# A PEER expert mixer on one core: the first head of the gathered tokens ranked in a batch of its own, its row gathers issued during the query projections, and three U blocks loaded there into a tile of their own

## The chip, the cores and the metric

The kernel runs on one core of a Trainium2 chip. The metric is the device time of one execution in microseconds (us). Engines: PE multiplies matrices, DVE (VectorE), ACT (ScalarE) and POOL (GpSimd) compute elementwise, SP only issues DMAs here. Each engine works through its instructions in the order in which they stand in its program; instructions on different engines wait for each other by semaphores.

## The reference, cut to what matters

The step handles 336 rows of width 1024: 256 prompt tokens, 64 sample tokens and 16 meta tokens. A trunk layer (convolution and state-space branches) comes first and is untouched by the change. Behind it 320 tokens go through a PEER mixer:

```python
def peer_block(xb, w_q, keys, U, V):
    q = (xb @ w_q).reshape(T, PEER_HEADS, 2, D_KEY // 2)       # 8 heads, 2 halves of 128
    s = jnp.einsum('thcd,hckd->thck', q, keys).astype(jnp.float32)   # 128 keys each
    s1, i1 = lax.top_k(s[:, :, 0], PEER_TOPK)                  # 16 best of each half
    s2, i2 = lax.top_k(s[:, :, 1], PEER_TOPK)
    cand = (s1[..., :, None] + s2[..., None, :]).reshape(T, PEER_HEADS, PEER_TOPK * PEER_TOPK)
    sc, f = lax.top_k(cand, PEER_TOPK)                         # 16 experts of 16384 per head
    ids = (jnp.take_along_axis(i1, f // PEER_TOPK, axis=-1) * N_KEYS
           + jnp.take_along_axis(i2, f % PEER_TOPK, axis=-1))
    g = jax.nn.softmax(sc, axis=-1)
    act = jax.nn.gelu(jnp.einsum('thkd,td->thk', U[ids], xb).astype(jnp.float32), approximate=False)
    w = (g * act).astype(xb.dtype)
    return jnp.einsum('thk,thkd->td', w, V[ids])
```

U and V have 16384 rows of 1024 floats, 64 MB each. Per token, 8 × 16 = 128 rows of each are used.

## The kernel before, in words

Two ways lead through the mixer, and both run at once.

**Gathered tokens.** The first 128 tokens (`NGAT`) fetch their own rows. A column is one of the 128 (head, rank) pairs; for each, one indirect DMA issued by POOL (line 1081) brings the row of U and V of every token, 128 × 2048 floats, into one of `UV` = 5 buffers named `wuv`. A *row look* (`pick_dot`, line 1193) is one DVE instruction that multiplies the U half with the token and sums it; ACT makes the Gelu of the sum and scales it (1195, 1196). A *row sum* (`pick_sum`, line 1201) is one DVE instruction that adds the scaled V half to `ygat`. 16 more columns hold the 16 meta tokens, so there are 144 gathers.

**Dense tokens.** The other 176 tokens (`ND`) go through all of U in 128 blocks of 128 experts: a 512 KB load by SP into a ring of eight buffers (`eraw`, line 1262), eight fp32 matmuls (`u_block`, line 1270; 16 matmul rows in the profile), a Gelu on ACT into `S` (1272). Then `S` is multiplied with gates, which PE builds from one-hot matrices (`pg`, `g_step`), and 128 blocks of V follow in the same manner (`va`, line 1364). The 16 choices of each of these tokens (the top-k of tiles 1 and 2, tile 2 with the meta tokens) are found by *background tasks* on DVE, mixed with the row looks while the U blocks run. At the end of a tile's ranking stands `look`, which ends in `pick` (line 1047); then PE transposes the picks (*placement*, `pix`, line 1161). A placement is tied behind a U block of a fixed number, `PLACE` = (38, 50) counted from 0.

**Before the blocks** come the 16 query projections, one per head and half (loop at line 1095): a 512 KB weight load, a cast `wh` on ACT (218), the rest `wl` on POOL (219), 24 matmuls, the copy `qT`, three score matmuls `psc` (1103) and copies of the scores (1105). DVE finds the 16 best of the gathered tokens at once (`top16`, line 995 ff.). `heads(h0)` then ranks the candidates of four heads in a batch of 26 DVE instructions and an Exp, and writes the row numbers `gid` and the weights `ggw`. Behind the first batch, with j = 7, `ahead(0)` issues the first gathers. The background top-k of tile 1 and 2 from score 6 on is tied behind the first batch's numbers (`early[0]`).

A scheduler with a simulated timeline decides the order in which each engine's instructions stand, from this recorded code, its waits and a few ties such as those of the placements. At the end, behind V block 126 (`LASTP`), `finish` normalises and writes the gathered tokens (`out_y`, line 1359), in tiles taken from the ring; `finish_dense` writes the others.

Of the kernel before, what the change touches and what calls it, by code (L numbers as in the profile page):

```python
# [7 lines left out]
F32 = mybir.dt.float32  # L8
# [13 lines left out]
PJ = 512  # L22
T = TP + NQ * TS
# [113 lines left out]
def body(tc, ia, oa, stop=None):  # L137
    nc = tc.nc
    with ExitStack() as top:
        cp = top.enter_context(tc.tile_pool(name="cp", bufs=1))  # L140
        ps = top.enter_context(tc.tile_pool(name="ps", bufs=1, space=bass.MemoryType.PSUM))
# [59 lines left out]
        def pj2(name="pj"):  # L201
            return pj(name)[:, :T2]
# [55 lines left out]
        def misc(shape, name):  # L258
            return ps.tile(shape, F32, name=name, tag="misc", bufs=2)
# [631 lines left out]
        for j in range(KD):  # L891
# [4 lines left out]
            p = pj2()  # L896
# [23 lines left out]
        p = ps.tile([128, T], F32, name="pn2", tag="pb", bufs=1)  # L920
# [9 lines left out]
        nd = gp.tile([128, KD, ND], F32, name="nd")  # L930
# [16 lines left out]
        kp = ks.enter_context(tc.tile_pool(name="kp2", bufs=1))  # L947
# [9 lines left out]
        for c_ in range(2):  # L957
            p = misc([128, 512], "px")
# [4 lines left out]
        p = misc([128, 4], "prs")  # L963
# [7 lines left out]
        if NX:  # L971
# [18 lines left out]
        keys = qp.tile([128, 16, NK], F32, name="keys")  # L990
# [14 lines left out]
        sv = [kp.tile([128, 16, 16], F32, name=f"sv{i}") for i in range(3)]  # L1005
        si = [kp.tile([128, 16, 16], U32, name=f"si{i}") for i in range(3)]
        sall = kp.tile([128, 2, 16, NK], F32, name="sall")
        cv0 = kp.tile([128, PH, 16], F32, name="cv0")
        ci0 = kp.tile([128, PH, 16], U32, name="ci0")

        def candidates(L, H_, s2):
            c = kp.tile([128, PH * 136], F32, name="cand", bufs=1)[:L]
            cf = c[:, :H_ * 136].rearrange("p (h n) -> p h n", h=H_)
            nc.vector.tensor_tensor(cf[:, :, :16], s2[:, :, 0, 0:1].to_broadcast([L, H_, 16]), s2[:, :, 1, :],
                                    op=OP.add)
            nc.vector.tensor_tensor(cf[:, :, 16:].rearrange("p h (a b) -> p h a b", b=8),
                                    s2[:, :, 0, 1:, None].to_broadcast([L, H_, 15, 8]),
                                    s2[:, :, 1, None, :8].to_broadcast([L, H_, 15, 8]), op=OP.add)
            return c, cf

        def table(L, H_, idx):
            sf = kp.tile([128, PH, 2, 16, 4], BF, name="sf", bufs=2)[:L, :H_]
            nc.vector.tensor_copy(sf.rearrange("p h c k t -> p (h c k) t"),
                                  idx.rearrange("p h k -> p (h k)")[:, :, None].to_broadcast([L, H_ * 32, 4]))
            return sf

        def places(L, H_, f):
            lo = kp.tile([128, PH * 16], U32, name="plo")[:L, :H_ * 16]
            rr = kp.tile([128, PH * 16], U32, name="prr")[:L, :H_ * 16]
            ab = [kp.tile([128, PH * 16], BF, name=f"pab{c_}")[:L, :H_ * 16] for c_ in range(2)]  # L1030
            nc.vector.tensor_scalar(lo, f, 7, None, op0=OP.bitwise_and)
            nc.vector.tensor_scalar(rr, f, 3, None, op0=OP.logical_shift_right)
            nc.vector.tensor_scalar(ab[0], rr, 1.0, 0.0, op0=OP.subtract, op1=OP.max)
            nc.vector.tensor_scalar(ab[1], rr, 1.0, 8.0, op0=OP.is_equal, op1=OP.mult)
            nc.vector.tensor_tensor(ab[1], ab[1], lo, op=OP.add)
            return ab

        def look(out, L, H_, at, sf, half, c):
            e = c.bitcast(BF)[:, :H_ * 256].rearrange("p (g a t) -> p g a t", a=16, t=4)
            nc.vector.tensor_tensor(e, at.rearrange("p (g t) -> p g t", t=4)[:, :, None, :].to_broadcast(  # L1040
                [L, H_ * 4, 16, 4]), iorep[:L, None, :16].to_broadcast([L, H_ * 4, 16, 4]), op=OP.is_equal)
            m = e.rearrange("p (h q) a t -> p h q (a t)", h=H_)
            nc.vector.tensor_tensor(m, m, sf[:, :, half].rearrange("p h k t -> p h (k t)")[:, :, None].to_broadcast(
                [L, H_, 4, 64]), op=OP.mult)
            for w in (8, 4, 2):
                nc.vector.tensor_tensor(e[:, :, :w], e[:, :, :w], e[:, :, w:2 * w], op=OP.add)  # L1046
            nc.vector.tensor_tensor(out.rearrange("p (g t) -> p g t", t=4), e[:, :, 0], e[:, :, 1], op=OP.add)

        early = []

        def heads(h0):
            hs_ = slice(h0, h0 + HG)
            cs = slice(16 * h0, 16 * (h0 + HG))
            sf = table(128, HG, si[0][:, 2 * h0:2 * h0 + 2 * HG])
            c, cf = candidates(128, HG, sv[0].rearrange("p (h c) k -> p h c k", c=2)[:, hs_])
            for h in range(HG):
                top16(cv0, ci0, cf[:, h], h0 + h)
            ab = places(128, HG, ci0.rearrange("p h k -> p (h k)")[:, cs])
            pk = kp.tile([128, 2, HG * 16], F32, name="pkh")
            for half in range(2):  # L1060
                look(pk[:, half], 128, HG, ab[half], sf, half, c)
            idf = kp.tile([128, HG * 16], F32, name="idh")
            nc.vector.scalar_tensor_tensor(idf, pk[:, 0], float(NK), pk[:, 1], op0=OP.mult, op1=OP.add)
            early.append(nc.vector.tensor_copy(gid[:, cs], idf).ins.name)
            g_ = kp.tile([128, HG, 16], F32, name="gh")
            nc.vector.tensor_tensor(g_, cv0[:, hs_], cv0[:, hs_, 0:1].to_broadcast([128, HG, 16]), op=OP.subtract)
            act(g_, g_, AF.Exp, scale=rsT[:, 0:1])
            sm = kp.tile([128, HG], F32, name="smh")
            nc.vector.tensor_reduce(sm, g_, axis=AX.X, op=OP.add)
            nc.vector.reciprocal(sm, sm)  # L1070
            nc.vector.tensor_tensor(ggw[:, cs].rearrange("p (h k) -> p h k", k=16), g_,
                                    sm[:, :, None].to_broadcast([128, HG, 16]), op=OP.mult)

        COLS = list(range(XAT)) + list(range(NPICK, NCOL)) + list(range(XAT, NPICK))
        pend = {}
# [1 line left out]
        ustep, vstep = [], []  # L1077

        def gather(c):
# [10 lines left out]
        def ahead(n):  # L1090
            for i_ in range(n, min(n + UV - 1, NCOL)):
                if i_ not in pend:
                    pend[i_] = gather(COLS[i_])

        for j in range(16):
            w = weight(ia["w_q"], j)
            p = pj()
            proj(p[:, :T2], w, rows(ah[:, :, :T2], al[:, :, :T2]))
            qT = qp.tile([128, T], F32, name="qT", bufs=3)
            nc.scalar.copy(qT[:, :T2], p[:, :T2])  # L1100
            p = misc([128, 3, NK], "psc")
            for i, (t0, L) in enumerate(KTILES):
                nc.tensor.matmul(p[:L, i], qT[:, t0:t0 + L], keys[:, j, :], start=True, stop=True)
                s_ = sall[:, i - 1, j] if i else kp.tile([128, NK], F32, name="sco", bufs=9)
                nc.scalar.copy(s_[:L], p[:L, i])
                if i == 0:
                    top16(sv[i], si[i], s_[:L], j)
            if j % (2 * HG) == 2 * HG - 1:
                heads(j // 2 - HG + 1)
            if j == 2 * HG - 1:  # L1110
                ahead(0)
        qs.close()
        xs.close()
        s0p = top.enter_context(tc.tile_pool(name="s0p", bufs=1, side=RIGHT))
# [145 lines left out]
        def block(src, i):  # L1260
            raw = ring()
            nc.sync.dma_start(raw, src[i])
            return raw.rearrange("p (k m) -> p k m", k=KD)

        def u_block(b):
            raw = block(ia["uT"], b)
            tag, nb = (("pj", 3), ("y", 2), ("pj", 3), ("y", 2), ("pj", 3), ("pb", 1))[b % 6]
            p = ps.tile([128, PJ], F32, name="pj", tag=tag, bufs=nb)[:, :T]
            for k in range(KD):
                i_ = nc.tensor.matmul(p[:, :ND], raw[:, k, :], nd[:, k, :], start=(k == 0), stop=(k == KD - 1))  # L1270
            ustep.append(i_.ins.name)
            nc.scalar.activation(Sv(b), p[:, :ND], AF.Gelu)  # L1272

        def after(i_, name):
# [223 lines left out]
```

## Time and profile before

| | |
|---|---|
| median of 3 runs | 1377.38 us (1375.13 to 1377.93) |
| the profiled execution's own time | 1379.1 us |
| its span in the profile | 1377.3 us |
| mean granted clock of PE | 0.988 |
| PE busy | 1317.0 us (96%) |
| DVE busy | 1015.0 us (74%) |
| ACT, POOL busy | 529.9, 580.0 us |
| moved by DMA | 382 MB, mean 277 GB/s |

All rows of a profile are of one execution; its own time is the one that sums are set against, and it stands 1.7 us above the median. The trunk fills the first 560 us or so, the query projections lie from about 560 to 655, the U blocks from there on, and the V blocks end at about 1365. Busy shares over the whole span say little here, since each stage has a limit of its own: windows of one stage, and the waits within it, are what to read.

### The profile page before, as it was taken

The numbers are of one execution on the slowest core, as the hardware profiler recorded it, in microseconds if no ns is written. First come the engines' busy times: TensorE is split into PE (matmuls) and PEld (weight loads), VectorE is DVE, ScalarE is ACT, GpSimd is POOL, SyncE is SP. The second block draws the span as 40 slices with busy tenths as digits, with TensorE's granted clock in tenths as the row PEclk, the third lists the DMA queues.
The fourth block names the chain that finished last, engine by engine and source line by source line (L and its number), as shares of the span: only waits on it lengthen the run. The fifth ranks groups of instructions, "written<-read, shape, count | busy, mean of one in ns | idle before, by whom it ended". The sixth has DMA issues, their size and how long they took to land.

```text
span 1377.3 us, 24605 instructions
## 1 busy us (share of the span) xinstructions
PE 1317.0 (96%) x9328; PEld 1244.9 (90%) x9328; DVE 1015.0 (74%) x2339; ACT 529.9 (38%) x1411; POOL 580.0 (42%) x477
## 2 busy tenths in 40 slices
PE   9899999999999999998998998999999999986997
PEld 7788888988889999898998998999999999976997
DVE  6787778877877246789999986668787777766533
ACT  6687877778666444343232221111111111111101
POOL 1386777776665667542212332123221212344210
PEclk9899999999999999999999999999999999999999
DMA  6435454444434544638999999899999999999993
GB/s 234 143 120 175 154 177 131 157 162 164 133 121 133 158 144 153 190 93 329 411 415 391 402 416 410 303 417 359 370 415 413 384 370 378 407 417 416 414 411 104
DMA packets 87094, 382.05 MB, mean 277 GB/s; under 512 B 10144, under 2 KB 15648, under 8 KB 66368
## 3 DMA queue, kind: packets, MB, share of 16 engines
q1 hardware_dynamic: 65056, 227.46, 45.9%
q0 software_dynamic: 20736, 151.00, 27.1%
q10 hardware_dynamic: 1184, 2.02, 0.4%
q8 instruction: 73, 1.20, 0.4%
q14 instruction: 45, 0.37, 0.1%
HBM read 367.41 MB, written 13.03 MB: 276 GB/s over the span
## 4 chain that ended last, share of the span: by engine, by line
PE 74%; DVE 14%; DMA 10%; ACT 1%; issue 0%; POOL 0%; DVEq 0%; ACTq 0%; SPq 0%; POOLq 0%
PE pj L151 31%; PE va L1364 17%; PE pj L1270 11%; DMA eraw<-in_vE_dram 7%; PE pg L1299 4%; DMA eraw<-in_uT_dram 3%; PE pst L151 2%; DVE ygat L1201 2%; DVE wuv L1193 2%; PE po L151 1%; PE py L151 1%; PE pdec L151 1%; PE ptr L156 1%; DVE cand L1046 1%; PE pq L151 1%; DVE si L1003 1%
## 5 line engine op out<-in xcount | busy, mean ns | idle before, releaser
L1081 POOL DMA_INDIRECT wuv<-in_peer_uv_dram,gid x144 | 187.7, 1303 | 513.2 <-DVE ygat L1201 149.1
L219 POOL TENSOR_TENSOR wl<-wraw,wh 128x1024 fp32r<-128x1024 f32 x111 | 267.0, 2407 | 178.0 <-ACT wh L218 96.6
L1364 PE MATMUL va<-S,eraw 128*128 128x176 f32 x2048 | 317.7, 315 | 19.9 <-DMA eraw<-in_vE_dram 19.9
L1364 PEld LDWEIGHTS va<-S,eraw 128*128 128x128 f32 x2048 | 306.0, 190 | 27.5 <-DMA eraw<-in_vE_dram 24.4
L1270 PE MATMUL pj<-nd,eraw 128*128 128x176 f32 x2048 | 318.9, 315 | 12.0 <-ACT S L1272 6.6
L1270 PEld LDWEIGHTS pj<-nd,eraw 128*128 128x128 f32 x2048 | 307.6, 191 | 15.1 <-ACT S L1272 9.3
L151 PE MATMUL pj<-ah,wh 128*128 128x336 f32 (+1 forms) x768 | 244.3, 329 | 2.5 <-ACT xg L194 2.2
L151 PE MATMUL pj<-al,wh 128*128 128x336 f32 (+1 forms) x768 | 234.4, 318 | 0.0
L1201 DVE SCALAR_TENSOR_TENSOR ygat<-wuv,scg,ygat 128x1024 f32<-128x1024 f32 x128 | 164.1, 1282 | 57.3 <-ACT scg L1196 57.1
L1195 ACT ACTIVATE scg<-scg 128x1 f32<-128x1 f32 x144 | 29.1, 202 | 420.0 <-DVE wuv L1193 419.9
L1193 DVE SCALAR_TENSOR_TENSOR wuv<-wuv,x2m 128x1024 f32<-128x1024 f32 x128 | 156.2, 1221 | 38.9 <-DMA wuv<-in_peer_uv_dram,gid 38.9
L218 ACT CAST wh<-wraw 128x1024 fp32r<-128x1024 f32 x125 | 131.3, 1051 | 119.0 <-PE pj L151 81.0
L472 DVE SCALAR_TENSOR_TENSOR pcv<-ccat,vec,pcv 128x256 f32<-128x256 f32 x464 | 148.9, 382 | 15.1 <-ACT pcv L470 15.1
L151 PEld LDWEIGHTS pj<-ah,wh 128*128 128x128 f32 x768 | 147.4, 192 | 10.4 <-issue 2.6
L151 PEld LDWEIGHTS pj<-al,wh 128*128 128x128 f32 x768 | 147.0, 192 | 0.7
L151 PE MATMUL pj<-ah,wl 128*128 128x336 f32 (+1 forms) x768 | 137.5, 316 | 0.0
L151 PEld LDWEIGHTS pj<-ah,wl 128*128 128x128 f32 x768 | 121.1, 189 | 0.9 <-issue 0.7
L1272 ACT ACTIVATE S<-pj 128x176 f32<-128x176 f32 x128 | 37.5, 312 | 145.0 <-PE pj L1270 145.0
L1299 PE MATMUL pg<-oh 128*128 128x64 bf16 x1056 | 74.9, 241 | 0.0
L1299 PEld LDWEIGHTS <-oh 128*128 128x128 bf16 x1056 | 70.8, 117 | 2.0
L1306 DVE TENSOR_TENSOR S<-S,pg 128x192 f32<-128x192 f32 (+1 forms) x66 | 31.6, 507 | 54.3 <-PE pg L1299 54.3
L486 DVE SCALAR_TENSOR_TENSOR pj<-mcat,vec,pj 128x360 f32<-128x360 f32 x96 | 56.6, 591 | 3.7 <-ACT pj L484 3.7
(363 smaller groups left out, 1709.4 us busy)
## 6 DMA issues: line engine op xcount, KB each, us to landing
eraw<-in_uT_dram SPq DMA_DIRECT2D x128, 512.0 KB, 11.0
eraw<-in_vE_dram SPq DMA_DIRECT2D x128, 512.0 KB, 11.7
wraw<-in_w_in_dram SPq DMA_DIRECT2D x80, 512.0 KB, 3.7
st<-in_state_dram SPq DMA_DIRECT2D x8, 1024.0 KB, 5.0
out_ssm_s_dram<-st SPq DMA_DIRECT2D x8, 1024.0 KB, 4.9
wraw<-in_w_mo_dram SPq DMA_DIRECT2D x16, 512.0 KB, 3.6
wraw<-in_w_q_dram SPq DMA_DIRECT2D x16, 512.0 KB, 3.6
wraw<-in_w_co_dram SPq DMA_DIRECT2D x8, 512.0 KB, 3.7
```

The lines of the kernel that those rows point to most:

```text
L151: i_ = nc.tensor.matmul(*a_, **kw)
L218: (nc.vector.tensor_copy if on_dve else nc.scalar.copy)(h, src)
L219: (nc.gpsimd if on_pool else nc.vector).tensor_tensor(l, src, h.bitcast(F32), op=OP.subtract)
L472: t = nc.vector.scalar_tensor_tensor(o, i_, wv, a_, op0=OP.mult, op1=OP.add)
L486: nc.vector.scalar_tensor_tensor(o, cat[:, w:w + n], wv, o, op0=OP.mult, op1=OP.add)
L1081: i_ = nc.gpsimd.indirect_dma_start(out=u, out_offset=None, in_=ia["peer_uv"], in_offset=bass.IndirectOffsetOnAxis(ap=gid[:, c:c + 1], axi ...
L1193: nc.vector.scalar_tensor_tensor(u[:, :D], u[:, :D], 1.0, x2m if c < NPICK else x2e, op0=OP.mult, op1=OP.mult, accum_out=w)
L1201: nc.vector.scalar_tensor_tensor(a_, u[:, D:], scg[:, c:c + 1], a_, op0=OP.mult, op1=OP.add)
L1270: i_ = nc.tensor.matmul(p[:, :ND], raw[:, k, :], nd[:, k, :], start=(k == 0), stop=(k == KD - 1))
L1272: nc.scalar.activation(Sv(b), p[:, :ND], AF.Gelu)
L1299: i_ = nc.tensor.matmul(pg[:, q, :], B[:, q // 4, :, q % 4], A[:, c_, q // 4, :, q % 4], start=(c_ == 0), stop=(c_ == 2))
L1364: i_ = nc.tensor.matmul(va[k // 2][:, k % 2], raw[:, k, :], Sv(b), start=False, stop=(b == 127), skip_group_check=True)
```

## The change

`heads` takes the number of heads as an argument, and the heads are ranked in three batches: head 0 alone behind projections 0 and 1, heads 1 to 3 behind projection 7, heads 4 to 7 at the end as before. The first gathers are issued behind the first batch, and the tie of the background top-k is to that batch's numbers too. Behind projection 6 three U blocks are loaded into a tile `pre` outside of the ring; their matmuls are recorded right behind the projections, tied behind the scores of projection 12, and `u_block` takes their result. What is computed is the same.

```diff
+BATCH = ((0, 1), (1, 3), (4, 4))
+NPRE = 3
+PREJ = 12
...
-        def heads(h0):
-            hs_ = slice(h0, h0 + HG)
-            cs = slice(16 * h0, 16 * (h0 + HG))
-            sf = table(128, HG, si[0][:, 2 * h0:2 * h0 + 2 * HG])
+        def heads(h0, n_):
+            hs_ = slice(h0, h0 + n_)
+            cs = slice(16 * h0, 16 * (h0 + n_))
+            sf = table(128, n_, si[0][:, 2 * h0:2 * h0 + 2 * n_])
...
+        def u_mm(b, raw):
+            tag, nb = (("pj", 3), ("y", 2), ("pj", 3), ("y", 2), ("pj", 3), ("pb", 1))[b % 6]
+            p = ps.tile([128, PJ], F32, name="pj", tag=tag, bufs=nb)[:, :T]
+            for k in range(KD):
+                i_ = nc.tensor.matmul(p[:, :ND], raw[:, k, :], nd[:, k, :], start=(k == 0), stop=(k == KD - 1))
+                if k == 0 and b < NPRE:
+                    tc.add_manual_dep(i_.ins, scored[PREJ], mybir.DependencyInfo(mybir.DependencyClass.NoSync,
+                                                                                 mybir.DependencyReason.DATA),
+                                      reason="behind the scores")
+            ustep.append(i_.ins.name)
+            return p
+
+        scored = []
+
+        us = ExitStack()
+        up = us.enter_context(tc.tile_pool(name="up", bufs=1))
         for j in range(16):
...
-            if j % (2 * HG) == 2 * HG - 1:
-                heads(j // 2 - HG + 1)
-            if j == 2 * HG - 1:
-                ahead(0)
+            for h0, n in BATCH:
+                if j == 2 * (h0 + n) - 1:
+                    heads(h0, n)
+                    if h0 == 0:
+                        ahead(0)
+            if j == 6:
+                pre = up.tile([128, NPRE, D], F32, name="pre")
+                for b in range(NPRE):
+                    nc.sync.dma_start(pre[:, b], ia["uT"][b])
+        early_u = [u_mm(b, pre[:, b].rearrange("p (k m) -> p k m", k=KD)) for b in range(NPRE)]
+        us.close()
...
         def u_block(b):
-            raw = block(ia["uT"], b)
...
+            p = early_u[b] if b < NPRE else u_mm(b, block(ia["uT"], b))
             nc.scalar.activation(Sv(b), p[:, :ND], AF.Gelu)
```

The scheduler turns this into other orders. **The first placement** on PE before: U blocks (`pj<-nd,eraw`), the three transposes, and the next blocks; `pick_8203` and `pick_8252` are the two halves of tile 1's picks.

```order
L1103 MATMUL psc<-keys,qT 128x128 x2
L1103 MATMUL psc<-keys,qT 64x128
L1270 MATMUL pj<-nd,eraw 128x176 x264
L1161 MATMUL pix<-cst,pick_8203 128x128
L1161 MATMUL pix<-cst,pick_8252 128x128
L1161 MATMUL pix<-cst,gsm 128x128
L1270 MATMUL pj<-nd,eraw 128x176 x96
```

And in the changed kernel, where line 1102 is `u_mm` and 1189 the placement:

```order
L1122 MATMUL psc<-keys,qT 128x128 x2
L1122 MATMUL psc<-keys,qT 64x128
L1102 MATMUL pj<-nd,eraw 128x176 x264
L1189 MATMUL pix<-cst,pick_8242 128x128
L1189 MATMUL pix<-cst,pick_8291 128x128
L1189 MATMUL pix<-cst,gsm 128x128
L1102 MATMUL pj<-nd,eraw 128x176 x96
```

Nothing moved: 39 blocks stand ahead of the first placement in both, and 12 more ahead of the second. On DVE the second half of the picks, `pick1`, stood like this before; rows with `wuv` and `x2m` are row looks, those with `ygat` row sums, those with `cand` the background ranking:

```order
L1193 SCALAR_TENSOR_TENSOR wuv_8101,scg_6613<-wuv_8101,x2m_6610 128x1024
L1046 TENSOR_TENSOR cand_7971<-cand_7971 128x32x32
L1046 TENSOR_TENSOR cand_7971<-cand_7971 128x32x16
L1201 SCALAR_TENSOR_TENSOR ygat_6609<-wuv_8101,scg_6613,ygat_6609 128x1024
L1046 TENSOR_TENSOR cand_7971<-cand_7971 128x32x8
L1047 TENSOR_TENSOR pick1_8252<-cand_7971 128x128
```

And now:

```order
L1221 SCALAR_TENSOR_TENSOR wuv_8399,scg_6613<-wuv_8399,x2m_6610 128x1024
L1049 TENSOR_TENSOR cand_8010<-cand_8010 128x32x16
L1049 TENSOR_TENSOR cand_8010<-cand_8010 128x32x8
L1229 SCALAR_TENSOR_TENSOR ygat_6609<-wuv_8399,scg_6613,ygat_6609 128x1024
L1050 TENSOR_TENSOR pick1_8291<-cand_8010 128x128
L1221 SCALAR_TENSOR_TENSOR wuv_8439,scg_6613<-wuv_8439,x2m_6610 128x1024
```

Counted from the start, the last look ahead of this pick is the 18th before and the 24th now, and the sums stand likewise; 26 more instructions of `heads`, for the third batch, are the only other difference up to there. Up to the second placement's last pick the looks are 24 and 30.

**The gathers** on POOL stood behind all weight subtractions (`wl`) of the projections before:

```order
L219 TENSOR_TENSOR wl<-wraw,wh 128x1024
L984 COPY xe<-xT 128x128 x4
L219 TENSOR_TENSOR wl<-wraw,wh 128x1024 x8
L1081 DMA wuv<-in_peer_uv_dram,gid 128x2048 x144
L1356 TENSOR_TENSOR wraw<-wraw,wuv 128x512
```

Now six of them stand between the last four:

```order
L987 COPY xe<-xT 128x128 x4
L222 TENSOR_TENSOR wl<-wraw,wh 128x1024 x4
L1084 DMA wuv<-in_peer_uv_dram,gid 128x2048 x5
L222 TENSOR_TENSOR wl<-wraw,wh 128x1024 x3
L1084 DMA wuv<-in_peer_uv_dram,gid 128x2048
L222 TENSOR_TENSOR wl<-wraw,wh 128x1024
L1084 DMA wuv<-in_peer_uv_dram,gid 128x2048 x138
```

So `wl` of projections 12 to 15 is computed behind the issue of the first gathers. **The last loads** on SP before, with the write of the gathered tokens (`out_y`):

```order
L1262 DMA eraw<-in_vE_dram 128x1024 x122
L953 DMA wuv<-in_fnorm_dram 128x1024
L1262 DMA eraw<-in_vE_dram 128x1024 x6
L1359 DMA out_y_dram<-wraw 128x512
L1359 DMA out_y_dram<-wraw 16x512
```

And now:

```order
L1290 DMA eraw<-in_vE_dram 128x1024 x120
L956 DMA wuv<-in_fnorm_dram 128x1024
L1290 DMA eraw<-in_vE_dram 128x1024 x7
L1382 DMA out_y_dram<-wraw 128x512
L1290 DMA eraw<-in_vE_dram 128x1024
L1382 DMA out_y_dram<-wraw 16x512
```

The last V block is loaded behind the first of these writes, and the first three U blocks no longer pass through the ring, so every later block takes a ring slot three further on.

More of the change, by code (lines that the diff above doesn't have):

```diff
@@ L1049, in body @@
         early = []
-        def heads(h0):
-            hs_ = slice(h0, h0 + HG)
-            cs = slice(16 * h0, 16 * (h0 + HG))
-            sf = table(128, HG, si[0][:, 2 * h0:2 * h0 + 2 * HG])
-            c, cf = candidates(128, HG, sv[0].rearrange("p (h c) k -> p h c k", c=2)[:, hs_])
-            for h in range(HG):
+        def heads(h0, n_):
+            hs_ = slice(h0, h0 + n_)
+            cs = slice(16 * h0, 16 * (h0 + n_))
+            sf = table(128, n_, si[0][:, 2 * h0:2 * h0 + 2 * n_])
+            c, cf = candidates(128, n_, sv[0].rearrange("p (h c) k -> p h c k", c=2)[:, hs_])
+            for h in range(n_):
                 top16(cv0, ci0, cf[:, h], h0 + h)
-            ab = places(128, HG, ci0.rearrange("p h k -> p (h k)")[:, cs])
-            pk = kp.tile([128, 2, HG * 16], F32, name="pkh")
+            ab = places(128, n_, ci0.rearrange("p h k -> p (h k)")[:, cs])
+            pk = kp.tile([128, 2, HG * 16], F32, name="pkh")[:, :, :n_ * 16]
             for half in range(2):
-                look(pk[:, half], 128, HG, ab[half], sf, half, c)
-            idf = kp.tile([128, HG * 16], F32, name="idh")
+                look(pk[:, half], 128, n_, ab[half], sf, half, c)
+            idf = kp.tile([128, HG * 16], F32, name="idh")[:, :n_ * 16]
             nc.vector.scalar_tensor_tensor(idf, pk[:, 0], float(NK), pk[:, 1], op0=OP.mult, op1=OP.add)
             early.append(nc.vector.tensor_copy(gid[:, cs], idf).ins.name)
-            g_ = kp.tile([128, HG, 16], F32, name="gh")
-            nc.vector.tensor_tensor(g_, cv0[:, hs_], cv0[:, hs_, 0:1].to_broadcast([128, HG, 16]), op=OP.subtract)
+            g_ = kp.tile([128, HG, 16], F32, name="gh")[:, :n_]
+            nc.vector.tensor_tensor(g_, cv0[:, hs_], cv0[:, hs_, 0:1].to_broadcast([128, n_, 16]), op=OP.subtract)
             act(g_, g_, AF.Exp, scale=rsT[:, 0:1])
-            sm = kp.tile([128, HG], F32, name="smh")
+            sm = kp.tile([128, HG], F32, name="smh")[:, :n_]
             nc.vector.tensor_reduce(sm, g_, axis=AX.X, op=OP.add)
@@ L1071, in heads @@
             nc.vector.tensor_tensor(ggw[:, cs].rearrange("p (h k) -> p h k", k=16), g_,
-                                    sm[:, :, None].to_broadcast([128, HG, 16]), op=OP.mult)
+                                    sm[:, :, None].to_broadcast([128, n_, 16]), op=OP.mult)
         COLS = list(range(XAT)) + list(range(NPICK, NCOL)) + list(range(XAT, NPICK))
@@ L1102, in body @@
             for i, (t0, L) in enumerate(KTILES):
-                nc.tensor.matmul(p[:L, i], qT[:, t0:t0 + L], keys[:, j, :], start=True, stop=True)
+                i_ = nc.tensor.matmul(p[:L, i], qT[:, t0:t0 + L], keys[:, j, :], start=True, stop=True)
+                if i == 0:
+                    scored.append(i_.ins.name)
                 s_ = sall[:, i - 1, j] if i else kp.tile([128, NK], F32, name="sco", bufs=9)
@@ L1265, in u_block @@
         def u_block(b):
-            raw = block(ia["uT"], b)
[L1267 to L1271, printed above, removed]
+            p = early_u[b] if b < NPRE else u_mm(b, block(ia["uT"], b))
             nc.scalar.activation(Sv(b), p[:, :ND], AF.Gelu)
```

## The prediction

> **What bounds the kernel now.** First the chain of waits by engine, which says that no single engine sets the whole span; then a table of windows that cuts the stretch which the change touches. Its columns are the stretch in us and its length, busy time (and instructions) of PE, PEld, DVE, ACT and POOL, granted clock, DMA share and GB/s.
>
> ```profile
> PE 74%; DVE 14%; DMA 10%; ACT 1%; issue 0%; POOL 0%; DVEq 0%; ACTq 0%; SPq 0%; POOLq 0%
> 579.50:734.10 154.60, 149.48 (x961) 143.30 (x961) 148.88 (x644) 48.88 (x149) 44.99 (x32) 0.97 0.80 310
> 734.10:770.10 36.00, 30.09 (x195) 28.95 (x195) 35.71 (x113) 8.11 (x26) 8.90 (x7) 1.00 0.98 382
> 770.10:860.00 89.90, 83.39 (x630) 81.54 (x631) 69.66 (x109) 17.17 (x74) 27.29 (x21) 1.00 1.02 414
> 860.00:1200.00 340.00, 340.00 (x2785) 336.21 (x2784) 255.90 (x406) 48.22 (x186) 81.17 (x67) 1.00 0.98 381
> 1200.00:1290.00 90.00, 70.58 (x441) 65.51 (x440) 58.64 (x70) 11.46 (x46) 35.55 (x21) 1.00 1.02 417
> ```
>
> From 579.5, where the first scores reach DVE, to 770.1, the end of the second placement, DVE works 148.88 of 154.60 us and then 35.71 of 36.00. PE is nearly as busy in the first stretch, but it has only 30.09 us of work in the 36.00 of the second. From 860 to 1200 PE is busy all the time. So before 770 DVE runs even with PE or ahead of it as the bound, and after 860 whatever PE lost stays lost.
>
> The two engines meet in the placements, where PE transposes what DVE picked (the end of a row in brackets is the idle time ahead of it, and what ended it):
>
> ```profile
> 725.70 7.32 PE L1270 MATMUL pj<-nd,eraw 128*128 128x176 f32 x48
> 732.86 0.27 PE L1161 MATMUL pix<-cst,pick 128*128 128x128 f32 x1
> 734.18 0.33 PE L1161 MATMUL pix<-cst,pick 128*128 128x128 f32 x1 [1.05 <-DVE pick L1047]
> 770.14 0.27 PE L1161 MATMUL pix<-cst,pick 64*128 64x64 f32 x1 [0.93 <-DVE pick L1047]
> 733.77 0.36 DVE L1047 TENSOR_TENSOR pick<-cand 128x128 f32<-128x128 bf16 x1
> 769.74 0.35 DVE L1047 TENSOR_TENSOR pick<-cand 64x128 f32<-64x128 bf16 x1
> ```
>
> PE waited only about 1 us at each place: 39 U blocks kept it just as long as DVE needed. **Anything that DVE gets to do ahead of these two picks therefore comes onto PE's path nearly in full**, since PE's order is fixed and the U blocks behind a placement can't pass it.
>
> **The change, part by part.** (a) *More rows ahead of the picks.* By the orders, DVE has 24 row looks and 24 row sums ahead of the second pick, 18 of each before; and 26 more instructions, since the heads are ranked in three batches instead of two over the same elements. Up to the second placement it is 30 against 24, so between the placements nothing is added. What a look and a sum cost in this stretch:
>
> ```profile
> 720.24 1.23 DVE L1193 SCALAR_TENSOR_TENSOR wuv<-wuv,x2m 128x1024 f32<-128x1024 f32 x1
> 721.38 1.23 DVE L1043 TENSOR_TENSOR cand<-cand,sf 128x2048 bf16<-128x2048 bf16 x1
> 722.52 1.29 DVE L1201 SCALAR_TENSOR_TENSOR ygat<-wuv,scg,ygat 128x1024 f32<-128x1024 f32 x1
> 723.72 1.15 DVE L1046 TENSOR_TENSOR cand<-cand 128x1024 bf16<-128x1024 bf16 x2
> ```
>
> From start to start a look takes 721.38 − 720.24 = 1.14 us and a sum 723.72 − 722.52 = 1.20, together 2.34; six pairs are 14.0 us. The 26 instructions have no new elements, so they cost the fixed part of an instruction each:
>
> ```profile
> L1046 DVE TENSOR_TENSOR cand<-cand 128x512 bf16<-128x512 bf16 x6 | 2.5, 421 | 0.1
> L1046 DVE TENSOR_TENSOR cand<-cand 128x256 bf16<-128x256 bf16 x6 | 1.7, 283 | 0.0
> 601.92 0.07 DVE L1003 MATCH_VALUE_LOAD si<-sv,sall 64x8 f32 x1
> ```
>
> Half the elements save 138 ns, so 283 − 138 = 145 ns is fixed; the shortest DVE row, 0.07, is the lower bound. 26 × 0.07 to 0.145 is 1.8 to 3.8 us. The added work is 15.8 to 17.8 us; I take 17. Some of it falls into DVE's idle time, which is 154.60 − 148.88 = 5.7 us in all:
>
> ```profile
> 587.83 0.29 DVE L995 MAX8 sv<-sco 128x8 f32<-128x128 f32 x1 [2.52 <-ACT sco L1105]
> 606.82 0.29 DVE L995 MAX8 sv<-sall 64x8 f32<-64x128 f32 x1 [1.54 <-ACT sall L1105]
> 630.31 1.15 POOL L1081 DMA_INDIRECT wuv<-in_peer_uv_dram,gid  x1 [6.68 <-DVE sv L995]
> DMA to landing us min/median/max: 8.4/8.4/8.4
> ```
>
> Head 0 is ranked across the gaps of 2.52 and 1.54 us. Against that its first rows take 8.4 us to land: with the numbers ready at about 607 (behind the rows that end before 606.82, plus the batch) they land at about 615, while only 27 DVE rows (at 0.2 to 0.3 us, some 7 us) stand between the numbers and the first look, which adds a wait of 1 to 2 us. Of the 5.7 I count 2 as regained, with 0 and 5.7 as bounds. **PE at both placements: 17 − 2 = +15 us late** (15.8 − 5.7 = 10.1 to 17.8), the first pick at about 749 instead of 734, the second at 785.
>
> (b) *The three early blocks.* They stand at the same place on PE as blocks 0 to 2 did. PE doesn't wait for a U block in the first stretch beyond its 154.60 − 149.48 = 5.1 us of idle time, and reaches the first placement with 15 us to spare now, so anything they save is waited away there: 0. That their 1.5 MB leaves the busy stretch counts under (d).
>
> (c) *Queues passed.* The first five gathers now stand ahead of four weight subtractions on POOL.
>
> ```profile
> 607.41 2.38 POOL L219 TENSOR_TENSOR wl<-wraw,wh 128x1024 fp32r<-128x1024 f32 x1 [1.89 <-PE pj L151]
> 614.22 0.45 PE L151 MATMUL pj<-ah,wl 128*128 128x320 f32 x2
> ```
>
> Five issues at 1.15 us are 5.8, and the subtraction that ended at 609.8 was used at 614.2, 4.4 us later: PE can be held by 1.4 us for it. Likewise ACT's first Gelu now stands ahead of the last copies of the projections. Both come ahead of the placement and lie in its 15 us of slack: 0. If (a) were gone, they would cost 0 to about 3 us.
>
> (d) *What comes back behind the second placement.* Six gathers that before came between there and about U block 93 are done, so DMA has less to carry. In 770 to 860 it was full (1.02, 414 GB/s), and PE lost there, by the list of waits (us, count, longest):
>
> ```profile
> PE pj L1270 <- DMA eraw<-in_uT_dram: 4.2, 3, 2.1
> PE pj L1270 <- ACT S L1272: 1.1, 1, 1.1
> PE pj L1270 <- ACT scg L1195: 0.9, 1, 0.9
> ```
>
> 6.2 us in all (0 to 6.2 can return). While PE stands at the placements the ring of eight blocks fills too, so I take **−5**. In 860 to 1200 PE has nothing to regain. The 90.00 − 70.58 = 19.4 us that PE loses from 1200 to 1290, with DMA full, stay: by the order the looks stand within one or two of their old V block from block 92 on, so the same bytes are left to move: 0.
>
> (e) *The clock behind the longer waits.* Nothing here shows 15 us of idle PE; the nearest is a short wait in the projections (windows: length, PE busy, clock, DMA share, GB/s):
>
> ```profile
> 651.63 0.43 PE L1103 MATMUL psc<-keys,qT 128*64 128x128 f32 x2 [2.74 <-ACT sall L1105]
> 652.00:654.00 2.00, 1.44 (x6) 0.51 1.00 412
> 654.00:656.00 2.00, 2.00 (x10) 0.64 0.99 408
> 656.00:658.00 2.00, 2.00 (x16) 1.00 1.05 430
> ```
>
> After 2.74 us without work the clock was 0.51 and 0.64 for some 4 us: 2 × (1 − 0.51) + 2 × (1 − 0.64) = 1.7 us lost. Where PE idles, the ground lost behind the first placement is made up ahead of the second, where PE has 5.9 us to spare; behind the second it stays. PE waits there less long, so 0 to 1.7, doubled for a longer wait 3.4; I take **+1.7**. The Trainium skill, "TensorE: Matmul & The Clock Gate", Part 1, says that half rate follows an idle window of about 3.4 us. By it the waits here, being longer, would all drop the clock; the row shows the drop after 2.74 already, and by either the sum is the same within 1.7 us.
>
> (f) *The end.* On SP the last V block's load now stands behind the write of the gathered tokens, which waits for DVE.
>
> ```profile
> wraw<-in_w_q_dram SPq DMA_DIRECT2D x16, 512.0 KB, 3.6
> 1355.17 0.43 DVE L1343 COPY wraw<-x2e 128x512 f32<-128x512 f32 x1 [3.61 <-issue]
> 1336.02 12.26 SPq L1262 DMA_DIRECT2D eraw<-in_vE_dram  x6
> 1359.04 2.69 SPq L1359 DMA_DIRECT2D out_y_dram<-wraw  x2
> 1365.26 0.32 ACT L1376 ACTIVATE sqd<-va 128x176 f32<-128x176 f32 x1 [6.28 <-PE va L1364]
> ```
>
> The write was issued at 1359.0; the finish takes its tiles from other ring slots, free one block (16 rows of a matmul at 7.32 / 48 = 0.15 us, 2.4 us) earlier, so at about 1356.7. A 512 KB load took 3.6 us where DMA was quiet, so the last block lands at 1361 to 1362; PE needs it one block ahead of 1365.2, at 1362.8. It just fits: 0, up to +2 if the write doesn't move.
>
> Sum: +15 − 5 + 1.7 + 0 = +11.7. The profiled execution took 1379.1 us (span 1377.3), so 1390.8; it is 1.7 above the median of the runs, 1377.4, beside which the forecast is **1389**. The low ends give 10.1 − 6.2 = +4, the high ends 17.8 + 3.4 + 2 = +23; they won't fall together, and 1382 to 1397 is the forecast's own range.
>
> **Rivals.** *DVE isn't late (faster, 0.12).* Busy time isn't all work:
>
> ```profile
> 617.44 1.51 DVE L1066 TENSOR_TENSOR gh<-cv 128x64 f32<-128x64 f32 x1
> ```
>
> 64 elements in 1.51 us, ten times the fixed cost, beside a busy POOL. If the earlier ranking and looks run over such stretches and fill all gaps, the looks that used to crowd 640 to 734 come early and DVE makes the first pick as before. Then only (d) is left: 1377.4 − 6.2 = 1371. It decides if the lateness is under 3 us (5 − 1.7); against it stands that 14.0 us of it are twelve instructions of known length in an order that can't be passed.
>
> *The loss is given back (same, 0.10).* A gather's size comes from the row of POOL's queue:
>
> ```profile
> q0 software_dynamic: 20736, 151.00, 27.1%
> ```
>
> 151.00 MB over 144 gathers are 1.05 MB each. While PE stands, DMA runs on. If the gathers get so far ahead that the 19.4 us of 1200 to 1290 shrink by the bytes of the six moved ones (6 × 1.05 MB at the 417 GB/s of that window are 15 us), the +12 vanish: 1377. It would need the lead of six looks to last to 1200; the order ends it at block 92.
>
> *Rows land late (slower still, 0.13).* The early gathers share DMA with the weights of the projections, and the fifth of the first five waits for the others: by 1.05 MB at 417 GB/s 2.5 us each, 10 us behind the first. If DVE, which can't pass a look, waits so for several, none of the idle time is regained and 4 to 8 us more come on top: +15 becomes 21 to 25, in all 1395 to 1399. The Trainium skill, "DMA: Bandwidth & Descriptors", section "Anatomy of one DMA — SWDGE (gpsimd) path", gives 2.0 us plus the bytes at 436 GB/s for one DMA, an estimate of 4.4 us for a row gather. By it the first look wouldn't wait, and the sum would be some 2 us lower; the measured 8.4 decides.
>
> **How the numbers follow.** Forecast 0.65, the rivals 0.12, 0.10 and 0.13. The range of 1376 to 1400 holds the forecast, the same and the slower case, and leaves out the faster one and the tails. Slower by over 0.2% (2.8 us, about what a measurement of this kernel can tell from no change) 0.78, within it 0.10, faster 0.12.
>
> **What will show it.** The first gather at about 607 instead of 630; PE waiting for a pick some 15 us at about 735 to 749, and again a few us at the second, at about 785; the waits for U blocks in the 90 us behind it gone; a clock below 1 behind both; the last V load behind the write. It is wrong if the pick comes before 740, if DVE waits over 5 us for rows ahead of it, or if PE's idle time from 1200 to 1290 changes.

## The result, and the profile after

| | before | changed |
|---|---|---|
| median | 1377.66 us (1375.13 to 1378.93, 4 runs) | 1388.21 us (1387.30 to 1389.82, 4 runs) |
| profiled execution, its span | 1379.1, 1377.3 us | 1389.8, 1388.1 us |
| PE busy | 1317.0 us | 1321.1 us |
| granted clock, mean | 0.988 | 0.979 |

The changed kernel takes 1.0075 times as long (95% interval 1.0062 to 1.0087): 10.5 us more. The size is the forecast's (1389); the way there is another.

The windows of the changed kernel, cut at the same events (first scores, ends of both placements), columns as in the prediction:

```profile
579.50:754.60 175.10, 152.30 (x964) 144.95 (x963) 173.76 (x689) 55.15 (x168) 55.29 (x39) 0.93 0.81 307
754.60:790.10 35.50, 31.18 (x196) 30.85 (x197) 35.29 (x113) 9.11 (x26) 11.10 (x7) 0.93 0.98 370
790.10:860.00 69.90, 68.54 (x486) 67.80 (x487) 50.15 (x78) 14.52 (x57) 24.73 (x15) 0.96 0.99 392
860.00:1200.00 340.00, 340.00 (x2819) 336.17 (x2818) 252.37 (x409) 47.40 (x179) 72.82 (x63) 1.00 0.96 376
1200.00:1290.00 90.00, 74.71 (x478) 70.99 (x478) 61.44 (x75) 12.43 (x50) 37.88 (x23) 1.00 1.02 416
```

The first stretch has grown from 154.6 to 175.1 us, the second has stayed. DVE is busy for 173.76 of the 175.10, 24.9 us more than before. PE isn't: it stands idle for 22.8 us there, where it did for 5.1. The placements in the changed kernel:

```profile
745.90 0.33 PE L1189 MATMUL pix<-cst,pick 128*128 128x128 f32 x1 [0.78 <-DVE pick L1050]
754.46 0.48 PE L1189 MATMUL pix<-cst,pick 128*128 128x128 f32 x1 [8.24 <-DVE pick L1050]
...
785.45 0.27 PE L1189 MATMUL pix<-cst,pick 64*128 64x64 f32 x1
790.04 0.37 PE L1189 MATMUL pix<-cst,pick 64*128 64x64 f32 x1 [4.32 <-DVE pick L1050]
```

The picks come 20.3 and 19.9 us later than before (734.18, 770.14), but PE waits only 0.78 + 8.24 + 4.32 = 13.3 us for them: it came late itself. Where, says the list of what PE waited for from 579 on (us in all, times, longest), first of the kernel before:

```profile
PE va L1364 <- DMA eraw<-in_vE_dram: 19.9, 20, 1.2
PE pj L1270 <- ACT S L1272: 6.6, 5, 2.0
PE pj L1270 <- DMA eraw<-in_uT_dram: 4.2, 3, 2.1
PE psc L1103 <- ACT sall L1105: 3.1, 2, 2.7
PE pix L1161 <- DVE pick L1047: 2.0, 2, 1.1
PE pj L1270 <- ACT scg L1195: 0.9, 1, 0.9
```

And of the changed one:

```profile
PE va L1387 <- DMA eraw<-in_vE_dram: 15.8, 15, 1.2
PE pix L1189 <- DVE pick L1050: 13.3, 3, 8.2
PE psc L1122 <- ACT sall L1126: 11.1, 4, 8.3
PE pj L1102 <- DMA eraw<-in_uT_dram: 2.6, 4, 1.1
...
PE pj L1102 <- ACT S L1295: 0.6, 1, 0.6
```

Against before: **+8.0 in the projections** (scores waiting for ACT's copies), **+11.3 at the picks**, −8.5 in the U blocks (loads, Gelus: 11.7 to 3.2), −4.1 at the V loads. That is +6.7 of idle time, and PE's busy time is 4.1 longer, since its clock fell to half behind the long waits; together the 10.8 us by which the spans differ. The wait of 8.3 us in the projections is this, in rows of PE, ACT and POOL:

```profile
625.84 1.42 PE L1122 MATMUL psc<-keys,qT 128*64 128x128 f32 x4 [8.30 <-ACT sall L1126]
625.10 0.20 ACT L1223 ACTIVATE scg<-scg 128x1 f32<-128x1 f32 x1 [9.19 <-DVE wuv L1221]
613.06 1.15 POOL L1084 DMA_INDIRECT wuv<-in_peer_uv_dram,gid  x1 [4.96 <-DVE si L1006]
```

The first gather went out at 613.06, not at about 607 as forecast, and ACT stood 9.2 us at the first row look's Gelu, with the copies of the scores behind it. Gather and look were late because DVE was held. DVE's rows:

```profile
601.07 0.27 DVE L1005 MAX8 sv<-sall 128x8 f32<-128x128 f32 x1
601.52 1.94 DVE L1043 TENSOR_TENSOR cand<-pab,iorep 128x256 bf16<-128x256 bf16 x1
605.82 2.35 DVE L1049 TENSOR_TENSOR cand<-cand 128x128 bf16<-128x128 bf16 x1
618.72 5.20 DVE L1017 TENSOR_TENSOR cand<-sv 128x48 f32<-128x48 f32 x1
637.33 2.92 DVE L1221 SCALAR_TENSOR_TENSOR wuv<-wuv,x2m 128x1024 f32<-128x1024 f32 x1
```

And POOL's at these times, all subtractions of the projections' weights:

```profile
600.93 2.38 POOL L222 TENSOR_TENSOR wl<-wraw,wh 128x1024 fp32r<-128x1024 f32 x1 [1.90 <-PE pj L154]
605.69 2.40 POOL L222 TENSOR_TENSOR wl<-wraw,wh 128x1024 fp32r<-128x1024 f32 x1 [2.38 <-ACT sall L1126]
...
619.22 4.64 POOL L222 TENSOR_TENSOR wl<-wraw,wh 128x1024 fp32r<-128x1024 f32 x2
...
635.57 3.59 POOL L222 TENSOR_TENSOR wl<-wraw,wh 128x1024 fp32r<-128x1024 f32 x1 [1.17 <-ACT scg L1224]
```

48 elements took 5.20 us, and end at 623.92 where POOL's two subtractions end at 623.86; the two rows above end at 603.46 and 608.17, POOL's at 603.31 and 608.09. The look at 637.33 ends at 640.25, about its own length behind POOL's end at 639.16. MAX8, which reads one operand, runs beside POOL in its usual 0.27 us. Six DVE rows of this kind lose 13.3 us up to the first placement (each against the shortest row of its shape); four of them, with 6.6 us, lie ahead of the first gather (one of 16 elements at 587.94 and one of 64 at 597.91 besides the two above). Before the change it was three rows and 3.9 us, among them the 1.51 us quoted in the prediction and this:

```profile
621.39 2.31 DVE L1071 TENSOR_TENSOR ggw<-gh,smh 128x64 f32<-128x64 f32 x1
```

The Trainium skill, "SBUF — State Buffer", section "SBUF: two separate sides", says that a DVE instruction with two inputs in SBUF and a GpSimd instruction that reads SBUF shut each other out for the whole instruction. The four rows agree in that each is held until POOL is done. The row of 5.20 us began 0.5 us ahead of the first of the two subtractions and was held through both all the same. Rows with one operand aren't all free of it: in the run with the gathers tied (below), a TENSOR_SCALAR and a CAST of 16 elements each took 2.09 and 2.27 us (L1034 at 586.76, L1067 at 614.52) and ended with POOL's subtraction. A ranking split off into the projections puts many such small instructions beside POOL's subtractions.

That the held row delays the look, and not the landing of the gathered rows, shows in the run without the early blocks (below), where the trace has the landing: issued at 612.67, the rows were in 5.5 us later, at 618.2, and DVE came to the look at 623.44:

```profile
618.33 5.18 DVE L1017 TENSOR_TENSOR cand<-sv 128x48 f32<-128x48 f32 x1
623.44 1.21 DVE L1221 SCALAR_TENSOR_TENSOR wuv<-wuv,x2m 128x1024 f32<-128x1024 f32 x1
```

### The profile page after: what moved, and what is told of

Read it like the earlier page. It is cut to its first block, busy times and chain, and to the rows that moved or that the text cites. A ratio compares the mean times of both kernels' runs of the same rounds, so it can differ in the third digit from the quotient of the medians.

```text
span 1388.1 us, 24636 instructions
## 1 busy us (share of the span) xinstructions
PE 1321.1 (95%) x9328; PEld 1252.6 (90%) x9328; DVE 1024.3 (74%) x2365; ACT 535.3 (39%) x1414; POOL 585.1 (42%) x477
## 4 chain that ended last, share of the span: by engine, by line
PE 81%; DVE 11%; DMA 5%; ACT 1%; issue 0%; POOL 0%; DVEq 0%; ACTq 0%; POOLq 0%
PE pj L154 31%; PE va L1387 20%; PE pj L1102 17%; PE pg L1322 5%; DMA eraw<-in_vE_dram 4%; PE pst L154 2%; DMA eraw<-in_uT_dram 1%; DVE wuv L1221 1%; DVE ygat L1229 1%; PE po L154 1%; PE py L154 1%; PE pdec L154 1%; DVE cand L1049 1%; PE ptr L159 1%; PE pq L154 1%; DVE cand L1043 1%
## 5 line engine op out<-in xcount | busy, mean ns | idle before, releaser
L1084 POOL DMA_INDIRECT wuv<-in_peer_uv_dram,gid x144 | 191.2, 1328 | 519.5 <-PE va L1387 115.9
L1387 PE MATMUL va<-S,eraw 128*128 128x176 f32 x2048 | 316.3, 314 | 15.8 <-DMA eraw<-in_vE_dram 15.8
L1387 PEld LDWEIGHTS va<-S,eraw 128*128 128x128 f32 x2048 | 306.1, 190 | 21.8 <-DMA eraw<-in_vE_dram 18.5
L1102 PE MATMUL pj<-nd,eraw 128*128 128x176 f32 x2000 | 313.2, 317 | 3.3 <-DMA eraw<-in_uT_dram 2.6
L1102 PEld LDWEIGHTS pj<-nd,eraw 128*128 128x128 f32 x2000 | 303.7, 193 | 5.2 <-issue 2.5
```

What stands on the lines that cost most here:

```text
L1084: i_ = nc.gpsimd.indirect_dma_start(out=u, out_offset=None, in_=ia["peer_uv"], in_offset=bass.IndirectOffsetOnAxis(ap=gid[:, c:c + 1], axi ...
L1387: i_ = nc.tensor.matmul(va[k // 2][:, k % 2], raw[:, k, :], Sv(b), start=False, stop=(b == 127), skip_group_check=True)
```

## The experiments

The theories: **A**, the row looks ahead of the picks make DVE late and PE waits for it (the prediction's step); **B**, ACT standing at the first Gelu in the projections; **C**, the early blocks and the shifted ring; and later **D**, POOL's subtractions hold the split ranking.

**One part undone at a time.** Without the early blocks:

```diff
-NPRE = 3
+NPRE = 0
```

> The changed kernel without the three early U blocks (all 128 through the ring), batches and early gathers as changed. By its order 23 and 29 row looks stand ahead of the two placements' last picks (changed kernel: 24 and 30; before: 18 and 24). Theory A, the row looks ahead of the picks set the loss: one look less is 2.3 us, 1385 to 1388. Theory B, ACT standing at the first Gelu in the projections (8.3 us) sets it: the Gelu still stands there, about 1388. Theory C, the early blocks and the moved ring set it: back to 1377 to 1379.

1389.32 us (1.0092 times before, 1.0069 to 1.0115). C falls. With the old batches and the early blocks kept:

```diff
-BATCH = ((0, 1), (1, 3), (4, 4))
+BATCH = ((0, 4), (4, 4))
```

> The changed kernel with the batches of before, (0, 4) and (4, 4), so the first gathers at their old place; the three early U blocks stay. 20 and 26 looks ahead of the two picks, two more than before. Theory A: up to 4.7 us over the kernel before less what comes back later, 1377 to 1381. Theory B: the Gelu is behind all but one of the projections' copies, 1377. Theory C: 1386 or more.

1375.91 us (0.9989, 0.9976 to 1.0003), a little under all that was expected. So the loss comes with the batches, and the early blocks alone cost nothing. PE waited 7.7 us for picks in this run, as theory A has it for two looks more, and lost nothing by it: the first sign against A.

With the gathers as late as before, but the ranking split:

```diff
+                    if h0 == 1:
+                        tc.add_manual_dep(tied[0], early[1], ...)   # first gather behind heads 1 to 3
```

> The changed kernel with its three batches and early U blocks, but the first gathers tied behind the second batch's row numbers (heads 1 to 3), as late as before. 16 and 23 looks ahead of the two picks, and the 26 instructions of the third batch. Theory A: two and one look less than before against 3 us of the batch, so 1374 to 1378. Theory B: no Gelu ahead of the projections' copies, 1377. If the third batch itself were the cost (its many small DVE instructions, some held by POOL): 1382 or more.

1388.42 us (1.0090, 1.0066 to 1.0114). A misses here: with fewer looks ahead of the picks than before, and no wait for any pick, the loss is the same; the third reading on record, that the batch itself costs, holds. ACT stood in the projections again, now at the Exp of the second batch, and PE 9.9 us behind it:

```profile
631.35 0.34 ACT L197 ACTIVATE gh<-gh,rsT 128x48 f32<-128x48 f32 x1 [12.73 <-DVE gh L1069]
```

With the Gelus of the first five looks behind the last copy of the projections:

```diff
+            if n < UV:
+                tc.add_manual_dep(i_.ins, qcopy[15], ...)   # i_: the Gelu
```

> The changed kernel with the Gelus of the first five row looks tied behind the last qT copy on ACT, so that ACT doesn't stand in the projections; gathers, looks and blocks as changed. 21 and 28 looks ahead of the two picks. Theory A: three and two looks fewer than the changed kernel, 5 to 7 us less, 1381 to 1384, with PE still waiting some 10 us for picks. Theory B: the 8 to 11 us are gone, 1377 to 1379, and no wait at the picks beyond that of before.

1388.42 us (1.0086, 1.0063 to 1.0108). A and B, in its narrow form, both miss: ACT no longer stands at the Gelu, but POOL does, at the first gather, waiting for DVE's row numbers, with the next weight subtraction behind it:

```profile
PE pj L154 <- POOL wl L222: 7.3, 1, 7.3
```

**Which wait costs?** The placements eight blocks later, so that PE never waits for a pick:

```diff
-PLACE = (38, 50)
+PLACE = (46, 58)
```

> The changed kernel with the placements eight U blocks later, behind blocks 46 and 58 instead of 38 and 50; batches, gathers, looks (24 and 30 ahead of the picks) as changed. If the loss is what PE waits at the picks (13.3 us in the changed kernel): those waits go, and 1376 to 1380 is left. If the loss is what PE lost ahead of U block 0 (8.3 us of ACT standing, blocks 0 to 2 some 11 us late) and the waits only show it again: 1385 to 1388.

1384.36 us (1.0044, 1.0029 to 1.0058), between the two: the waits at the picks are gone, yet 15.5 us of waits for U loads and Gelus have come up, and PE stood 7.4 us at one place in the projections (8.3 in the changed kernel). So the 13.3 us at the picks were worth some 4 us at most, about 2 of which are the shorter waits in the projections (8.9 against 11.1). Gathers and Exp both tied (the edits of the third run, and the second batch's Exp behind the last copy):

> The changed kernel with the first gathers tied behind the second batch's numbers, and the Exp of the second batch (for which ACT stood 12.7 us in the run with the gathers tied alone, with PE waiting 9.9) tied behind the last qT copy. Three batches and early U blocks as changed; 16 and 22 looks ahead of the picks. If an in-order engine that waits for DVE in the projections is the cost: PE is on time, 1375 to 1379. If the third batch costs in another way: 1385 or more.

1389.63 us (1.0083, 1.0064 to 1.0102). A miss: the tie moved the stand to the next such place. The last score copies now stood behind a Gelu that waited 13.53 us, PE 11.8:

```profile
658.02 0.20 ACT L1231 ACTIVATE scg<-scg 128x1 f32<-128x1 f32 x1 [13.53 <-DVE wuv L1229]
```

**Is POOL the cause?** The subtractions left out on both kernels:

```diff
-            w = weight(ia["w_q"], j)
+            w = weight(ia["w_q"], j, lows[j % 2] if j > 3 else None)   # low part of projection 2 or 3
```

> The changed kernel without the subtractions wl of query projections 4 to 15: the low parts of projections 2 and 3 are multiplied again in their place, so the matmuls, loads and casts are the same and POOL is free but for the gathers. 23 and 29 looks ahead of the picks. Theory D, DVE's small instructions of the split ranking stand behind POOL's subtractions (1.94, 2.35 and 5.20 us in the changed kernel): these rows fall to 0.2 us, no stand of 8 us on PE, and the time is within 5 us of the run without wl on the old kernel. If the stands come from the order alone, they stay, and the difference stays near 10 us.

> The kernel before, with the same subtractions left out (low parts of projections 2 and 3 multiplied again). 18 and 24 looks ahead of the picks. The partner of the run above: 1374 to 1378 by either theory.

1371.33 us for the changed kernel (0.9959, 0.9945 to 0.9973) and 1373.30 for the old one (0.9959, 0.9947 to 0.9972; a little under the 1374 expected): no difference that the intervals can tell, where it was 10.5 us. PE waited 13.1 us at the picks of the first, with five looks more ahead of them, and it cost nothing. DVE's rows of the shapes that had taken 5.20 and 1.94 us, here grouped by shape (count, busy, mean ns):

```profile
L1046 DVE TENSOR_TENSOR cand<-pab,iorep 128x256 bf16<-128x256 bf16 x2 | 0.5, 270 | 0.0
...
L1020 DVE TENSOR_TENSOR cand<-sv 128x48 f32<-128x48 f32 x1 | 0.2, 177 | 0.0
```

Then with everything computed, the subtractions of projections 8 to 15 on DVE:

```diff
-            split(h, l, raw, on_pool=not on_dve, on_dve=lm[0] == 1)
+            split(h, l, raw, on_pool=not (on_dve or dve), on_dve=lm[0] == 1)   # dve: j > 7
```

> The changed kernel with the subtractions wl of query projections 8 to 15 on DVE instead of POOL (1.22 us each there against 2.4 on POOL, so 9.8 us more DVE work), everything computed. 22 and 29 looks ahead of the picks, two and one fewer. Theory D: some 10 of the 13.5 us that DVE rows lost beside POOL's subtractions go, so DVE does more and is still not later; with the two looks fewer it is about 5 us earlier at the picks, 1380 to 1386. If the time DVE's rows took there was not POOL's doing: 5 us later, 1388 to 1394.

1376.53 us (0.9990, 0.9980 to 0.9999): better than theory D had it, the whole loss gone, with 9.8 us more work on the busy engine. No DVE row is held any more up to the first placement: 13.3 us of holds and 4.7 of two looks and sums less, against the 9.8, make 8.2 us, and the first placement was done 9 us ahead of the changed kernel's (745.1 against 754.5). The list of PE's waits in this run:

```profile
PE va L1387 <- DMA eraw<-in_vE_dram: 18.5, 18, 1.2
PE pix L1189 <- DVE pick L1050: 12.9, 2, 8.4
PE pj L1102 <- DMA eraw<-in_uT_dram: 1.3, 2, 1.1
PE psc L1122 <- ACT sall L1126: 0.7, 2, 0.4
```

The waits at the picks are as long as in the changed kernel (13.3). What is missing is the stand in the projections, 0.7 against 11.1, and the half clock behind it: PE is busy 1316.1 us instead of 1321.1. But this run doesn't show that free DVE rows alone remove the stand, since the scheduler's order is another one as well. The first gather, the first look and its Gelu:

```profile
619.35 1.14 POOL L1084 DMA_INDIRECT wuv<-in_peer_uv_dram,gid  x1 [41.29 <-DVE sv L998]
627.30 1.22 DVE L1221 SCALAR_TENSOR_TENSOR wuv<-wuv,x2m 128x1024 f32<-128x1024 f32 x1
628.94 0.20 ACT L1223 ACTIVATE scg<-scg 128x1 f32<-128x1 f32 x1
```

Gather and look come later than in the changed kernel (613.06, 623.85), yet ACT doesn't stand: 34 of its 48 score copies lie ahead of this Gelu, 24 did there. In the run without `wl` the place is nearer to the changed kernel's, 28 copies ahead, and there the look comes 10.5 us earlier, at 613.37.

The control, the same edit on the kernel before:

> The kernel before with the subtractions wl of query projections 8 to 15 on DVE instead of POOL, as in the run on the changed kernel that came to 1376.5. 18 and 24 looks ahead of the picks, as before. Theory D: only the split ranking stands behind POOL's subtractions; the kernel before lost 3.9 us beside them against 9.8 us of added DVE work, so DVE is some 6 us later at the picks, 1378 to 1384. If the move of the subtractions is a gain in itself, whatever the ranking: 10 us less here too, 1367 to 1371.

1382.00 us (1.0034, 1.0020 to 1.0047). So the move is no gain in itself; it costs where the ranking isn't split.

**Better versions.** The old batches with the early blocks, and the placements later by four:

> The three early U blocks with the batches of before, and the placements four U blocks later (behind 42 and 54). With the placements at 38 and 50 PE waited 7.7 us for the picks there. If those waits cost time: they go, 1370 to 1374. If U loads or Gelus take their place, as they did in part where the changed kernel was placed eight blocks later: 1375 to 1377, no better than the old batches alone (1375.9).

1379.11 us (1.0006, 0.9995 to 1.0017), above both expectations; and by eight:

> The same with the placements eight U blocks later (46 and 58). If the waits for picks cost time: 1370 to 1374, as with four blocks, since four already cover them. If other waits take their place: 1375 to 1378.

1374.92 us (0.9983, 0.9973 to 0.9994), just under the second one. In both the waits at the picks were gone and others had come up, 13.8 and 12.0 us in the U blocks, as the second theory has it. The first is no better than the kernel before; the second is barely faster than the kernel before, and so is the changed one with `wl` on DVE; of the versions that compute everything no other is, and these two are so by 0.1 to 0.2%.

All runs side by side; the columns are PE's waits in us by the lists of each profile (projections: for ACT's copies and POOL's `wl`; U blocks: loads and Gelus), and the ratio to the kernel before:

| run | projections | picks | U blocks | V loads | ratio |
|---|---|---|---|---|---|
| before | 3.1 | 2.0 | 11.7 | 19.9 | 1 |
| changed | 11.1 | 13.3 | 3.2 | 15.8 | 1.0075 |
| no early blocks | 13.1 | 13.9 | 1.4 | 19.0 | 1.0092 |
| gathers tied | 11.5 | 0 | 13.5 | 19.6 | 1.0090 |
| Gelus behind | 8.0 | 7.4 | 8.8 | 20.4 | 1.0086 |
| placements +8 | 8.9 | 0 | 15.5 | 15.4 | 1.0044 |
| gathers and Exp tied | 13.6 | 0 | 14.1 | 19.2 | 1.0083 |
| old batches | 2.2 | 7.7 | 2.4 | 19.6 | 0.9989 |
| old batches, placements +4 | 2.2 | 0 | 13.8 | 19.6 | 1.0006 |
| old batches, placements +8 | 2.2 | 0 | 12.0 | 20.5 | 0.9983 |
| changed, `wl` on DVE | 0.7 | 12.9 | 1.9 | 18.5 | 0.9990 |
| before, `wl` on DVE | 0.7 | 9.4 | 8.3 | 19.1 | 1.0034 |
| changed, no `wl` | 1.9 | 13.1 | 0.6 | 17.1 | 0.9959 |
| before, no `wl` | 0.4 | 0.4 | 12.8 | 20.6 | 0.9959 |

Two things are to be seen. Waits at the picks and in the U blocks stand in for each other: their sum lies between 10 and 18 us in every row, so a microsecond at a pick is mostly one that a load or a Gelu would have taken. And all six runs with 8 us or more in the projections are slower by 0.4 to 0.9%; of the others only one is, by 0.3%, the one whose sum of the two is the largest (17.7).

The table goes by what PE waited for, and that is not yet a proof. In the changed kernel the stand lies ahead of a pick that PE has to wait for as well, so that without it PE would have waited longer there: which of the two carries the loss can't be told from that kernel alone. The runs with no wait at a pick (gathers tied, gathers and Exp tied) show that the stand can be enough for all of it; old batches and the runs without `wl` show that waits at the picks can cost nothing.

## Why the prediction was right in size and wrong on the way

**Rows ahead of the picks (a).** That DVE comes late at the picks was right; the size was off, +20.3 us at the first instead of +15. DVE's 24.9 us of added busy time are the 14.0 of the six looks and sums, about 9.4 of rows held by POOL (13.3 against 3.9), and 1.5 left for the 26 instructions, a little under the bound of 1.8. Its idle time fell by 4.4 us (5.7 to 1.3), not by 2. The step that failed here is the price of the ranking's instructions: 0.07 to 0.145 us, taken from rows in which POOL isn't subtracting. The row of 1.51 us that showed the other price was quoted, under a rival, as time that could be regained.

**"Comes onto PE's path nearly in full".** Up to the placements it did: PE was 20.3 and 19.9 us late there. Behind them it failed: 10.8 us were left at the end, 9.1 came back where 5 less 1.7 of clock were forecast. Counted in waits, 11.3 us more at the picks came, and 12.6 went in the U blocks and at the V loads; three runs with 7.7 to 13.1 us at the picks are not slower than their partners (old batches, `wl` on DVE, no `wl`). A likely reason is that DMA was full while PE waited (1.02 and 414 GB/s from 746 to 756), so that loads came ahead for which PE doesn't wait later. No run tests it by itself, and DMA was as full during the stand in the projections (0.99 and 406 GB/s from 616 to 626), which by the table wasn't made up for; why not stays open.

**Queues passed (c).** Taken as 0 within the slack of the placements; PE lost 8.0 us there, and by the table this is the part that stays. The Gelu ahead of the copies was named, but "0 to about 3" counted one weight subtraction behind five gather issues; it didn't see that the Gelu would wait for a look that is itself behind a held DVE row. Whichever in-order engine was freed by a tie, the next one stood (ACT at a Gelu, at an Exp, POOL at a gather). What counts is how late DVE is against the place that the scheduler gave to the instruction which waits for it: with `wl` on DVE the look was later still, its Gelu stood further back, and nothing was lost.

**What comes back (d).** −5 was forecast for the U blocks, −8.5 measured. The V loads were to stay at 19.4; they gave back 4.1, and a change of PE's idle time from 1200 to 1290 (it fell to 90.00 − 74.71 = 15.3) was one of the prediction's own signs of being wrong. Why, the runs don't show: without the early blocks they gave back only 0.9, with the same batches.

**The clock (e).** +1.7 forecast, and PE's busy time grew by 4.1. Behind the second pick's wait, the columns being length, PE busy, clock, DMA share, GB/s:

```profile
790.00:792.00 2.00, 1.96 (x7) 0.50 1.04 430
792.00:794.00 2.00, 2.00 (x8) 0.50 1.01 416
794.00:796.00 2.00, 2.00 (x9) 0.50 0.77 260
796.00:798.00 2.00, 2.00 (x15) 0.98 1.01 401
```

6 us at half clock lose 3.0 here; the stretches behind the first pick and behind the stand in the projections add to it.

**The early blocks (b) and the end (f)** came as forecast. The early blocks alone (old batches) are within 0.3% of before. The last V load does stand behind the write, and PE has no wait for it:

```profile
1367.32 0.34 SPq L1382 DMA_DIRECT2D out_y_dram<-wraw  x1
1368.21 0.33 SPq L1290 DMA_DIRECT2D eraw<-in_vE_dram  x1
1369.65 0.35 SPq L1382 DMA_DIRECT2D out_y_dram<-wraw  x1
```

So the forecast of +11.7 met the 10.8 between the spans by luck, with errors that balance. On PE's path: some 5 us more lateness at both placements than the +15, and 5.8 more given back than the 5 less 1.7. In terms of waits: 8.0 in the projections and 2.4 of clock not foreseen, 7.6 more coming back than foreseen, and 3.7 less at the picks than the lateness forecast for them.

**What stays open.** How the scheduler came to put the Gelu and the Exp ahead of the copies wasn't tried. No run changes the held rows and keeps the order, so how the loss divides between the two isn't shown. The run with `wl` on DVE beat its expectation of 1380 to 1386 in part because all of the holds went, where some 10 us of them were expected to; the rest may lie in its other order.

## What to carry to other kernels

Before small DVE instructions are moved earlier, look at what POOL does at that place: a row there can cost what POOL's instructions still have to run, not its elements, and every in-order engine that waits for it passes the delay on to work that has nothing to do with it. Look also at where the instruction that waits for it stands in its own engine's order. Where a stretch is bound by transfers, a new wait at one place can be taken from the others, so add up all of an engine's waits over the stretch before calling one of them the loss. And a total that comes out right does not confirm its terms.

## What the runs showed of the hardware

Not expected was how little work can hold DVE how long: 48 elements for 5.20 us beside two POOL subtractions in a row, 0.18 to 0.20 us without them. The same subtraction takes 2.4 us on POOL and 1.22 on DVE. And a longer wait doesn't mean a longer stretch at half clock: PE worked at half for some 6 us behind waits of 4.3 and 8.3 us, and for some 4 behind waits of 2.74 and 8.24.
